# Gated channels one step ahead in a two-layer trunk: a change to the order of work in the first layer

## The chip, the cores and the metric

The kernel runs on one core of one Trainium2 chip. The metric is the device time of one execution in microseconds (us), lower is better. A run of this kernel gives one such time; the median of three runs stands for the kernel. One further execution was recorded with the hardware profiler, and all rows below come from it. Engine names follow the profile: PE is the matrix engine (PEld its weight loads), DVE the vector engine, ACT the scalar engine, POOL and SP the two others; SP issues most transfers and POOL issues the accumulating ones.

## The reference

The program is a trunk of two layers over 256 latent tokens and 256 context tokens of 1024 channels. Cut to what matters here, one layer does this:

```
h  = modulate(rmsnorm(x, norm1_g[l]), sh1, sc1)      # shifts and scales from silu(c) @ w_ada[l]
p  = h @ w_in[l]                                     # GLU columns | q k v | branch gates
u  = a * sigmoid(g)                                  # a, g: the two halves of the GLU columns
u  = dwconv1d(u, dw, dw_b)                           # depthwise, 31 taps, 512 channels
y_conv = silu(layernorm(u, ln_g, ln_b)) @ w_conv_out
y_attn = neighbourhood_attention(rope(q), rope(k), v, k_ctx, v_ctx, rpb) @ w_na_out
x  = x + g1 * ((sigmoid(pg_c) * y_conv + sigmoid(pg_a) * y_attn) @ w_out)
h2 = modulate(rmsnorm(x, norm2_g[l]), sh2, sc2)
x  = x + g2 * conv_ffn(h2)
```

The context tokens go through the same weights in the first layer with their own modulation and plain attention; in the second layer only their keys and values are needed. Weights and activations are float32. The kernel keeps that precision by splitting each operand into a high part and the rest and adding three products.

## The kernel before, in words

Channels lie on the 128 partitions and tokens on the free axis, 512 columns in the first layer (latent and context side by side). A **group** is one output tile of 128 channels: `group` runs over eight input tiles of 128 channels and `mm3` (lines 196 to 199) issues three matmuls for each, so a group is 24 matmuls into one of four PSUM banks tagged `main`. Its weights are one unit of 512 KB. `unit8` brings a unit in by one of two ways. `wadded` (lines 211 to 219) loads it on SP, lets ACT make the high part `whi` (line 216) and its negative `wlo` (217), and adds the loaded unit to that by an accumulating DMA from POOL (218). `wunit` (lines 157 to 180) lets ACT make `whi` (167) and DVE subtract it (168). A table at the top of the file, `ADDED`, says which unit goes which way; gates 5 and 7 of the first layer are not in it. There are four buffers each for the loaded unit (`raw`), `whi` and `wlo`.

The first layer's front runs in this order. Groups for the first GLU pair (which stand in two `sc` banks) and for the values end near 57 us. Then come, for each of four **pairs** of heads, a query group and a key group (`qk`, line 843), three further GLU pairs of two groups each (`glu_groups`, line 701), and sixteen gate groups (`gate`, line 708). After a query or key group DVE applies the rotary table (lines 859 to 869), ACT writes the high part (881) and DVE the low part (882). After a GLU pair ACT takes the tanh (691) and DVE the product (693), and 31 convolution **taps** per pair join a list; a tap is one DVE instruction over 512 columns (671 the first, 673 the others).

What is interleaved is set by generators. `group` calls `slot()` at its middle and at its end, and each slot advances every generator in `side`: `conv_run` (line 677) issues `rate` taps a slot; `Attention.run` steps the attention; `ada_dots` (line 289) issues the row sums, here called **dots**, that make the later modulation vectors: one DVE instruction over 128x1024 (line 304) for each of two token streams and each tile of `w_ada`, `pace` dots a slot. `layer_norm` (line 938) drains the taps, then sums the four channel tiles (949 to 951), has PE form the mean (955), and so on to the normal form (966 to 969).

The attention of a pair has three parts on PE: the scores (495), the transposes of the probabilities (561), and the values (578, 587). DVE takes the bias and the maximum (516), ACT the exponential (519) and the scaling (522); ACT copies the transposes out of PSUM (564, 567 for context). Latent scores of pair 0 are here called scores 0, and so on. `glu_groups(j)` calls `att.ahead(j - 2)`, which makes the attention issue the scores of all pairs up to that number; `qk(j)` does the same. A scheduler places the instructions of each engine in an order from this recording; each engine then runs its own list strictly in that order.

After the attention the tiles of its pool are free, and two 512 KB rows and the first `own` tiles for the dots are loaded into that space. The remaining gates follow, then eight half groups for the attention branch (`branch(U_NA, ...)`, DVE line 993), eight for the convolution branch (998, 999 and 1001 on DVE, 1000 on ACT) whose result `z` (tiles `h`) is the input of the output groups at line 1033. The dots of lines 933 and 1052 must be complete before the second norm.

Of the kernel before, what the change touches and what calls it, by code (L numbers as in the profile page):

```python
# [53 lines left out]
def trunk(ctx: ExitStack, tc: tile.TileContext, xt, cvec, crow, wall, wada, params, bias_t, rope_t, out):  # L54
# [13 lines left out]
    def nm(s):  # L68
        uid[0] += 1
        return f"{s}_{uid[0]}"  # L70
# [6 lines left out]
    def tmp(w=512):  # L77
        return tp.tile([P, w], F32, tag="t", bufs=5, name=nm("t"))
# [10 lines left out]
    def add_side(gen):  # L89
        side.append(gen)  # L90
# [196 lines left out]
    pace = [1.0]  # L287
# [344 lines left out]
    for l in range(DEPTH):  # L632
        last = l == DEPTH - 1
# [4 lines left out]
        with ExitStack() if last else start as e1a:  # L638
# [36 lines left out]
            rate = [0.0]  # L675
# [22 lines left out]
            def in_group(t, c, tag="main"):  # L698
                return group(psum(tag), unit8(l, U_IN + t), *h1, c)

            def glu_groups(j):
                pa = in_group(T_GLU + 2 * (j - 1), ALL)
                pg = in_group(T_GLU + 2 * (j - 1) + 1, ALL)
                copied = None if last else att.ahead(j - 2)
                with tc.issue_after(copied.ins) if copied else ExitStack():
                    glu(j, pa, pg)

# [5 lines left out]
            with ExitStack() as e1b:  # L713
# [3 lines left out]
                att = Attention(l, eb, T, V, VW, oh, ol, after)  # L717
# [125 lines left out]
                def qk(j):  # L843

                    att.ahead(j - 2)
                    bt = eb.tile([P, 5, NS_ // 2], F32, tag="bias", bufs=2 if last else 1, name=nm("bias"))
                    both = []
                    for what in range(2):
                        w = T if what == 0 else 2 * S
                        sc = HD ** -0.5 if what == 0 else 1.0  # L850
                        ps = in_group((T_Q, T_K)[what] + j, slice(0, w))
                        if what == 0:
                            with tc.issue_after(lastdma[0].ins):
                                sp.dma_start(bt, bias_t[l, j])
                        r1, r2 = tmp(), tmp()
                        got = back(ps[:, :w])
                        lat, ctx_ = (got[:, 0], got[:, 1]) if w > S else (got, None)
                        part = halves if w == S else lambda a: a
                        dve.tensor_tensor(part(r1[:, LAT]), lat, part(rope[:, 0, :]), ALU.mult)
                        dve.stream_shuffle(part(r2[:, LAT]), lat, SWAP16)  # L860
                        dve.tensor_tensor(r2[:, LAT], r2[:, LAT], rope[:, 1, :], ALU.mult)
                        if what == 0:
                            rq = tmp()
                            dve.tensor_tensor(
                                rq[:, LAT].rearrange("p (b r c) -> p b r c", b=NB_, r=ROWS),
                                blocks(r1[:, LAT]), blocks(r2[:, LAT]), ALU.add,
                            )
                        else:
                            dve.tensor_tensor(r1[:, LAT], r1[:, LAT], r2[:, LAT], ALU.add)
                        f = eb.tile([P, 2, KN if what else w], F32R, tag="qk"[what], bufs=2, name=nm("qk"))  # L870
                        if what == 0:
                            to = [([f[:, a, LAT] for a in range(2)], rq[:, LAT])]
                            if T > S:
                                to.append(([f[:, a, CTX] for a in range(2)], ctx_))
                        else:
                            rv_ = r1[:, LAT].rearrange("p (r c) -> p r c", r=ROWS)
                            to = [([f[:, a, KCTX] for a in range(2)], ctx_)]
                            for d, c in ((slice(0, KL), slice(GW - TC, GW)), (slice(KX, KN), slice(0, TC))):
                                to.append(([f[:, a, d].rearrange("p (c r) -> p r c", r=ROWS) for a in range(2)], rv_[:, :, c]))
                        for (hi, lo), src in to:  # L880
                            act.activation(hi, src, AF.Identity, scale=sc)
                            end = dve.scalar_tensor_tensor(lo, src, sc, hi.bitcast(F32), ALU.mult, ALU.subtract)  # L882
                        both.append(f)
                    att.pair(j, *both, bt, end)

                if l == 0:
                    for t in range(4):
                        keep_v(t, pv[t])
                    qk(0)
                    arun = att.run()  # L890
                    add_side(arun)
                    for j in range(1, 4):
                        glu_groups(j)
                        qk(j)
                        rate[0] = 3
                else:
                    glu_groups(2)
                    rate[0] = 3
                    wvs = [wunit(l, U_V + uu) for uu in range(4)]
                    for half in range(2):  # L900
                        pv = {t: psum() for t in (2 * half, 2 * half + 1)}
                        for k in range(KD):
                            v_tile(pv, wvs[k // 2], k, pv)
                            if k % 2:
                                slot()
                        for t, p in pv.items():
                            keep_v(t, p)
                    qk(0)
                    glu_groups(3)
                    arun = att.run()  # L910
                n = 0
                if last:
                    add_side(arun)
                    for j in range(1, 4):
                        gate(ea, n)
                        n += 1
                        qk(j)
                while att.busy() and n < (14 if last else 5):
                    gate(ea, n)
                    n += 1  # L920
                while att.busy():
# [3 lines left out]
            with ExitStack() as e1c:  # L925
                ec = e1c.enter_context(tc.tile_pool(name=f"ec{l}", bufs=1))

                if l == 0:
                    sb0 = [across(ec, s) for s in range(2)]

                    own = lambda: ec.tile([P, UW], F32, tag="own", bufs=4, name=nm("own"))
                    pace[0] = 0.5
                    g1 = ada_dots(0, range(16, 40), sb0, own, 2)
                    add_side(g1)
                sh_ = [ec.tile([P, T], F32R, name=f"sh{l}_{j}") for j in range(KC)]
# [2 lines left out]
                def layer_norm():  # L938

                    while taps:  # L940
                        for _ in range(6 if last else 5):
                            if taps:
                                conv_tap(*taps.pop(0))
                        yield
                    pace[0] = 1.0 if last else 1.2
                    flat = [c.rearrange("p s t -> p (s t)") for c in cb]
                    sm = tp.tile([P, 512], F32, tag="ss", name=nm("ss"))
                    eng = pool if last else dve
                    eng.tensor_tensor(sm[:, :T], flat[0], flat[1], ALU.add)
                    eng.tensor_tensor(sm[:, :T], sm[:, :T], flat[2], ALU.add)  # L950
                    dve.tensor_tensor(sm[:, :T], sm[:, :T], flat[3], ALU.add)
                    for _ in range(1 if last else 5):
                        yield
                    pm = psum("po")
                    pe.matmul(pm[:, :T], one.to_broadcast([P, P]), sm[:, :T], start=True, stop=True)
                    (s2,) = sum_squares(1, T)
                    for j in range(KC):
                        dve.scalar_tensor_tensor(flat[j], pm[:, :T], -1.0 / CONV, flat[j], ALU.mult, ALU.add)
                        s2.add(flat[j], j == KC - 1)
                    for _ in range(2 if last else 5):  # L960
                        yield
                    pb = yield from rstd(s2, CONV, "po", 0 if last else 2)
                    for j in range(KC):
                        sg = tmp()
                        g, b = pr(l, LNG + j, 1), pr(l, LNB + j, 1)
                        dve.scalar_tensor_tensor(flat[j], flat[j], g, pb[:, :T], ALU.mult, ALU.mult)
                        act.activation(sg[:, :T], flat[j], AF.Silu, bias=b)
                        act.copy(sh_[j], sg[:, :T])
                        dve.tensor_tensor(sl_[j], sg[:, :T], sh_[j].bitcast(F32), ALU.subtract)
                        yield  # L970
                    if last:
                        pace[0] = 0.4
# [384 lines left out]
```

## Time and profile before

| what | value |
|---|---|
| three runs | 1054.67, 1055.67, 1056.23 us |
| median | 1055.67 us |
| profiled execution, own time | 1054.58 us |
| its span, first to last instruction | 1052.8 us |
| PE, DVE, ACT busy in the span | 1032.4, 893.2, 565.6 us |
| taps (673) / dots (304) in the whole program | 240 / 128 |

The profiled execution's own time is 1.8 us above its span and 1.09 us below the median. In the page a group of instructions is one line of code on one engine with output and input tile names; a row of the timeline gives start, duration, engine, line, tiles and, in square brackets, how long the engine stood idle before it and what ended that. A 512-column matmul is recorded as 379 to 386 ns long, although one starts every 0.22 us: matmuls overlap, so PE's busy time hides short stalls.

### The profile page before, as it was taken

The page shows a single profiled execution, that of the slowest core. Times are in us where ns is not written, and L with a number is a line of the kernel's source. Part 1 is how long each engine was busy: PE and PEld are TensorE (multiplying, and loading weights), DVE is VectorE, ACT ScalarE, POOL GpSimd, SP SyncE. Part 2 cuts the span into 40 slices and gives each one's busy share as a digit, 9 for nine tenths or more (in the row PEclk, how much of TensorE's full clock was granted, in tenths as well). Part 3 has the DMA queues.
Part 4 walks back from the last instruction along what each step waited for, and adds up shares of the span by engine and source line. Part 5 has one row for each costly group of instructions (what it writes and reads, how often), then busy time and mean ns, then how long its engine had stood idle before and what let it go on. Part 6 is the DMA issues. An engine that isn't in the chain of part 4 may idle for free.

```text
span 1052.8 us, 17991 instructions
## 1 busy us (share of the span) xinstructions
PE 1032.4 (98%) x6886; PEld 932.9 (89%) x6886; DVE 893.2 (85%) x1608; ACT 565.6 (54%) x921; POOL 43.7 (4%) x59
## 2 busy tenths in 40 slices
PE   9999999999999999999999999999999999999997
PEld 7787788888889988888888889999889999999996
DVE  6568899999998787878788888799899988988883
ACT  4458768545434644444444223545777666766652
POOL 1111110011000000000000000000000000000000
PEclk9999999999999999999999999999999999999998
DMA  9989674888945345454545887556734485666781
GB/s 374 305 221 229 156 181 121 258 255 236 305 146 177 104 140 160 140 164 143 166 145 160 301 289 249 180 189 209 208 123 135 161 292 176 193 201 199 221 283 57
DMA packets 59511, 209.26 MB, mean 199 GB/s; under 512 B 7201, under 2 KB 7457, under 8 KB 59425
## 3 DMA queue, kind: packets, MB, share of 16 engines
q1 hardware_dynamic: 54384, 190.77, 55.3%
q0 software_dynamic: 4752, 17.30, 8.7%
q8 instruction: 54, 0.88, 0.3%
q14 instruction: 33, 0.26, 0.1%
q10 hardware_dynamic: 288, 0.04, 0.0%
HBM read 187.63 MB, written 1.05 MB: 179 GB/s over the span
## 4 chain that ended last, share of the span: by engine, by line
PE 68%; DVE 17%; ACT 5%; DMA 4%; issue 3%; SPq 1%; DVEq 0%; ACTq 0%
PE main L197 20%; PE main L198 20%; PE main L199 20%; DVE cb L673 6%; PE main L736 4%; DVE wlo L168 3%; DMA raw<-in_wall 2%; DVE t L304 2%; DMA own<-in_wada 1%; SPq L728 1%; PE sc L197 1%; PE sc L199 1%; PE sc L198 1%; DVE qk L882 1%; ACT pp L519 1%
## 5 line engine op out<-in xcount | busy, mean ns | idle before, releaser
L197 PE MATMUL main<-h,whi 128*128 128x256 f32 (+1 forms) x1328 | 433.1, 326 | 1.2 <-DVE qk L882 1.2
L198 PE MATMUL main<-h,whi 128*128 128x256 f32 (+1 forms) x1328 | 430.2, 324 | 0.9 <-DVE h L1001 0.7
L199 PE MATMUL main<-h,wlo 128*128 128x256 f32 (+1 forms) x1328 | 429.9, 324 | 1.2 <-DVE wlo L168 1.1
L167 ACT CAST whi<-raw 128x1024 fp32r<-128x1024 f32 (+1 forms) x211 | 218.3, 1039 | 234.8 <-PE main L198 173.6
L168 DVE TENSOR_TENSOR wlo<-raw,whi 128x1024 fp32r<-128x1024 f32 (+1 forms) x211 | 253.6, 1208 | 67.2 <-ACT whi L167 66.4
L197 PEld LDWEIGHTS main<-h,whi 128*128 128x128 f32 x1328 | 252.8, 190 | 22.0 <-issue 1.3
L199 PEld LDWEIGHTS main<-h,wlo 128*128 128x128 f32 x1328 | 252.5, 190 | 18.5 <-DVE wlo L168 1.8
L198 PEld LDWEIGHTS main<-h,whi 128*128 128x128 f32 x1328 | 252.7, 190 | 18.3 <-DVE h L1001 1.0
L304 DVE CUSTOM_DVE_ANT_0 t<-own,sb,par 128x1024 bf16<-128x1024 f32 x120 | 151.8, 1282 | 6.8 <-DMA own<-in_wada 6.8
L673 DVE SCALAR_TENSOR_TENSOR cb<-u,par,cb 128x512 f32<-128x512 f32 (+1 forms) x240 | 144.7, 620 | 2.8
L198 PE MATMUL main<-fl,whi 128*128 128x256 f32 (+1 forms) x396 | 122.8, 310 | 0.0
L197 PE MATMUL main<-fh,whi 128*128 128x256 f32 (+1 forms) x396 | 122.8, 310 | 0.0
L199 PE MATMUL main<-fh,wlo 128*128 128x256 f32 (+1 forms) x396 | 122.5, 310 | 0.0
L197 PEld LDWEIGHTS main<-fh,whi 128*128 128x128 f32 x396 | 75.6, 191 | 3.8 <-ACT fh L1095 0.2
L198 PEld LDWEIGHTS main<-fl,whi 128*128 128x128 f32 x396 | 75.6, 191 | 3.7 <-DVE fl L1096 0.2
L199 PEld LDWEIGHTS main<-fh,wlo 128*128 128x128 f32 x396 | 75.5, 191 | 3.6
L216 ACT CAST whi<-raw 128x1024 fp32r<-128x1024 f32 x33 | 34.6, 1049 | 36.0 <-PE main L198 30.5
L404 ACT ACTIVATE h<-t,mod 128x256 fp32r<-128x256 f32 x56 | 25.2, 503 | 34.8 <-DVE t L403 34.3
L218 POOL DMA_DIRECT2D wlo<-raw x33 | 28.9, 877 | 258.9 <-ACT wlo L217 107.6
L736 PE MATMUL main<-whi,h 128*128 128x512 f32 x128 | 38.5, 386 | 0.2
L1105 ACT ACTIVATE t<-t 128x512 f32<-128x512 f32 x22 | 13.9, 632 | 41.3 <-DVE t L1074 41.3
L217 ACT ACTIVATE wlo<-whi 128x1024 fp32r<-128x1024 f32 x33 | 35.0, 1061 | 0.5
(214 smaller groups left out, 1268.8 us busy)
## 6 DMA issues: line engine op xcount, KB each, us to landing
raw<-in_wall SPq DMA_DIRECT2D x240, 512.0 KB, 4.3
own<-in_wada SPq DMA_DIRECT2D x72, 512.0 KB, 4.7
wlo<-raw POOLq DMA_DIRECT2D x33, 512.0 KB, 5.4
raw<-in_wada SPq DMA_DIRECT2D x16, 512.0 KB, 5.8
bias<-in_bias_t SPq DMA_DIRECT2D x8, 520.0 KB, 5.3
row<-in_wada SPq DMA_DIRECT2D x8, 512.0 KB, 5.1
sb<-in_crow SPq DMA_DIRECT2D x5, 512.0 KB, 4.8
x<-in_xt SPq DMA_DIRECT2D x4, 512.0 KB, 5.1
```

The source lines that it names most:

```text
L167: act.copy(hi[:, c], r[:, c])
L168: dve.tensor_tensor(lo[:, c], r[:, c], hi[:, c].bitcast(F32), ALU.subtract)
L197: pe.matmul(ps, w[0], order(xh), start=start, stop=False)
L198: pe.matmul(ps, w[0], order(xl), start=False, stop=False)
L199: pe.matmul(ps, w[1], order(xh), start=False, stop=stop)
L216: act.copy(hi, r)
L217: act.mul(lo, hi.bitcast(F32), -1.0)
L218: pool.dma_start(lo, r, accum_op=ALU.add)
L304: dve.tensor_tensor_reduce(tmp().bitcast(BF16), r, v, 1.0, pr(l, BADA + n, 1), ALU.mult, ALU.add, mods[l][:, n, s : s + 1])
L404: high = act.activation(hi[:, c], y[:, c], AF.Identity, bias=b)
L673: dve.scalar_tensor_tensor(cb[j], src, w, cb[j], ALU.mult, ALU.add)
L736: mm = pe.matmul(pv[t], h1[n == 1][k][:, c], runs(w[n == 2][:, b]), start=k + n == 0, stop=k == KD - 1 and n == 2)
```

## The change

The first layer's order is altered in four ways, and the second layer's order is left as it is.

- GLU pair j+1 is computed ahead of query and key pair j: `glu_groups(1)` stands before `qk(0)`, and the loop runs `glu_groups(j + 1)` and `qk(j)` for j = 1, 2. `glu_groups` asks for the scores only up to pair j - 3. The last pair's queries and keys come behind the first gate, by the loop that the second layer used before.
- The taps go at three a slot beside GLU groups, two beside the queries and keys of pairs 2 and 3, one beside pair 1, and three beside pair 0. Before it was two up to the end of pair 1 and three after.
- Up to eight gates, not five, are taken while the attention is unfinished.
- The pace of the dots is 0.8 a slot, not 0.5, until the taps are drained, and 1.4, not 1.2, from there to the attention branch.

```diff
             def glu_groups(j):
                 pa = in_group(T_GLU + 2 * (j - 1), ALL)
                 pg = in_group(T_GLU + 2 * (j - 1) + 1, ALL)
-                copied = None if last else att.ahead(j - 2)
+                copied = None if last else att.ahead(j - 3)
...
                     att.ahead(j - 2)
+                    if not last:
+                        rate[0] = 1.0 if j == 1 else 2.0 if j else 3.0
...
                     att.pair(j, *both, bt, end)
+                    rate[0] = 3.0
...
+                    rate[0] = 3.0
+                    glu_groups(1)
                     qk(0)
                     arun = att.run()
                     add_side(arun)
-                    for j in range(1, 4):
-                        glu_groups(j)
+                    for j in range(1, 3):
+                        glu_groups(j + 1)
                         qk(j)
-                        rate[0] = 3
...
-                    for j in range(1, 4):
+                for j in range(1 if last else 3, 4):
+                    if True:
                         gate(ea, n)
                         n += 1
                         qk(j)
-                while att.busy() and n < (14 if last else 5):
+                while att.busy() and n < (14 if last else 8):
...
-                    pace[0] = 0.5
+                    pace[0] = 0.8
...
-                    pace[0] = 1.0 if last else 1.2
+                    pace[0] = 1.0 if last else 1.4
```

The change adds five lines up to there, so line 881 of before is line 883 of after, and 1001 is 1006. Three places show what it does to the engines' lists.

On ACT, the place is the stretch around the first pair's queries. Line 216 makes the high part of a weight unit, 217 its negative, 881 (883) the high part of queries or keys `qk`, 691 a tanh. Before:

```order
L216 CAST whi_897<-raw_895 128x1024
L217 ACTIVATE wlo_898<-whi_897 128x1024
L881 ACTIVATE qk_716<-main_672 128x256
L881 ACTIVATE qk_716<-t_714 128x256
L216 CAST whi_946<-raw_944 128x1024
L217 ACTIVATE wlo_947<-whi_946 128x1024
L881 ACTIVATE qk_763<-main_721 128x256
L881 ACTIVATE qk_763<-t_757 128x4x40 x2
L216 CAST whi_1028<-raw_1026 128x1024
```

The same place now, from the same ordinal unit (`raw_854` is the fifth of this run, as `raw_895` was) to the seventh and eighth:

```order
L216 CAST whi_856<-raw_854 128x1024
L217 ACTIVATE wlo_857<-whi_856 128x1024
L216 CAST whi_894<-raw_892 128x1024
L691 ACTIVATE t_747<-main_709 128x512
L217 ACTIVATE wlo_895<-whi_894 128x1024
L216 CAST whi_984<-raw_982 128x1024
L883 ACTIVATE qk_797<-main_751 128x256
L217 ACTIVATE wlo_985<-whi_984 128x1024
L883 ACTIVATE qk_797<-t_795 128x256
L216 CAST whi_1031<-raw_1029 128x1024
```

The high part of pair 0's queries stood ahead of the sixth unit and pair 0's keys ahead of the seventh; now both stand behind the cast of the seventh unit, `raw_982`. On SP the seventh load of this run stands, before and now, behind sixteen small transfers of line 728.

On PE, the place is the start of the output groups (line 1033). Their input `z` is eight tiles of 128 channels, each with a high and a low part, all named `h`. In before the last tile's parts are `h_2676` and `h_2684`, and `main_3044` and `main_3079` are the first and the second output group. Before, behind seven tiles of the first group and eleven matmuls of the second:

```order
L197 MATMUL main_3079<-h_2672,whi_3081 128x512
L198 MATMUL main_3079<-h_2680,whi_3081 128x512
L197 MATMUL main_3044<-h_2676,whi_3046 128x512
L199 MATMUL main_3079<-h_2672,wlo_3082 128x512
L197 MATMUL main_3079<-h_2673,whi_3081 128x512
L198 MATMUL main_3079<-h_2681,whi_3081 128x512
L199 MATMUL main_3079<-h_2673,wlo_3082 128x512
L197 MATMUL main_3079<-h_2674,whi_3081 128x512
L198 MATMUL main_3044<-h_2684,whi_3046 128x512
L199 MATMUL main_3044<-h_2676,wlo_3047 128x512
```

Now, where `main_3038` is the first output group and the last tile's parts are `h_2655` and `h_2663`:

```order
L197 MATMUL main_3038<-h_2654,whi_3040 128x512
L198 MATMUL main_3038<-h_2662,whi_3040 128x512
L199 MATMUL main_3038<-h_2654,wlo_3041 128x512
L197 MATMUL main_3038<-h_2655,whi_3040 128x512
L198 MATMUL main_3038<-h_2663,whi_3040 128x512
L199 MATMUL main_3038<-h_2655,wlo_3041 128x512
L197 MATMUL main_3079<-h_2648,whi_3081 128x512
L198 MATMUL main_3079<-h_2656,whi_3081 128x512
L199 MATMUL main_3079<-h_2648,wlo_3082 128x512
```

Before, the last low part was wanted by the 39th matmul of the output groups; now it is wanted by the 23rd, straight behind the seventh tile.

On DVE, the place is the end of the chain that makes those parts: line 998 (1003) multiplies a convolution group by its gate, 999 (1004) adds the attention branch, 1001 (1006) is the low part, 304 a dot and 168 the low part of a weight unit. Before:

```order
L1001 SCALAR_TENSOR_TENSOR h_2683<-t_3014,h_2675 128x512
L998 SCALAR_TENSOR_TENSOR t_3038<-g_7_2288,main_3019 128x512
L304 ISA t_3110,mod_105<-own_2963,sb_2143,par 128x1024
L304 ISA mod_105 128x1
L999 TENSOR_TENSOR t_3038<-t_3038,g_15_2667 128x512
L304 ISA t_3112,mod_105<-own_2963,sb_2146,par 128x1024
L304 ISA mod_105 128x1
L1001 SCALAR_TENSOR_TENSOR h_2684<-t_3038,h_2676 128x512
```

Now:

```order
L1004 TENSOR_TENSOR t_3014<-t_3014,g_14_2597 128x512
L168 TENSOR_TENSOR wlo_3082<-raw_3080,whi_3081 128x1024
L1003 SCALAR_TENSOR_TENSOR t_3032<-g_7_2274,main_3019 128x512
L1006 SCALAR_TENSOR_TENSOR h_2662<-t_3014,h_2654 128x512
L1004 TENSOR_TENSOR t_3032<-t_3032,g_15_2646 128x512
L304 ISA t_3057,mod_105<-own_2889,sb_2215,par 128x1024
L304 ISA mod_105 128x1
L1006 SCALAR_TENSOR_TENSOR h_2663<-t_3032,h_2655 128x512
```

Of the 48 dots that stand ahead of the second norm in both kernels, 40 stood ahead of the last low part before, and 37 do now. Ahead of the centred tiles of the layer norm (line 958, now 963) it was 6 and is 8, ahead of the normal form (966, now 971) 18 and 20; so 22 dots stood between the normal form and the last low part, and now 17.

Counted on PE, the mean of the layer norm (line 955, now 960) and all that follows it stands one and a half groups, 36 matmuls, later among the gate groups, so that as much less gate work lies between that mean and the output groups. From the second norm on, the lists of the two kernels agree.

## The prediction

> **What bounds the kernel now.** I read the page first.
>
> ```profile
> span 1052.8 us, 17991 instructions
> PE 1032.4 (98%) x6886; PEld 932.9 (89%) x6886; DVE 893.2 (85%) x1608; ACT 565.6 (54%) x921; POOL 43.7 (4%) x59
> ```
>
> PE is the bound, and the change gives it neither more nor fewer instructions. So the time can move only where PE waits or starts late. The second view is the table of stretches, cut at the layer's stages. Its columns are the stretch, its length, then busy time and count of PE, PEld, DVE, ACT and POOL, the granted clock, the share of the DMA engines and GB/s.
>
> ```profile
> 57.60:97.00 39.40, 38.02 (x201) 32.19 (x199) 31.66 (x72) 27.80 (x47) 6.83 (x8) 1.00 0.89 226
> 97.00:156.00 59.00, 56.60 (x396) 46.98 (x397) 54.12 (x119) 43.48 (x92) 6.93 (x8) 1.00 0.74 176
> 156.00:196.40 40.40, 40.27 (x289) 33.58 (x288) 36.93 (x66) 29.96 (x67) 2.62 (x3) 1.00 0.54 146
> 196.40:238.10 41.70, 40.73 (x191) 35.10 (x190) 38.75 (x59) 18.49 (x24) 4.63 (x4) 1.00 0.90 274
> 238.10:296.90 58.80, 58.14 (x271) 50.20 (x270) 56.05 (x89) 26.45 (x33) 5.26 (x6) 1.00 0.83 248
> 296.90:322.70 25.80, 25.80 (x177) 24.19 (x175) 23.01 (x49) 8.74 (x16) 0.00 (x0) 1.00 0.40 124
> 322.70:1052.80 730.10, 717.32 (x5011) 667.49 (x5009) 621.49 (x1077) 382.69 (x593) 10.36 (x15) 1.00 0.59 186
> 400.00:420.00 20.00, 20.00 (x94) 17.51 (x93) 16.49 (x24) 9.07 (x12) 0.00 (x0) 1.00 0.51 152
> ```
>
> From 57.6 to 296.9 us, where all moved work lies, PE idles 1.38 + 2.40 + 0.13 + 0.97 + 0.66 = 5.5 us: that is about all that better order can win. The last row is the measure of PE's step: 94 matmuls of 512 columns in 20.00 us, 0.213 each; with a few records missing I take 0.216, so a group of 24 is 5.2 us. DVE, at 80 to 95 per cent, is what PE waits for. The waits themselves are in PE's timeline:
>
> ```profile
> 96.04 0.44 PE L495 MATMUL sc<-qk,qk 64*128 64x416 f32 x2 [0.87 <-ACT qk L881]
> 97.07 0.62 PE L495 MATMUL sc<-qk,qk 64*128 64x416 f32 x4 [0.58 <-DVE qk L882]
> 104.61 0.27 PE L561 MATMUL pt<-ident,pp 64*128 64x64 f32 x1 [0.25 <-ACT pp L522]
> 128.60 1.28 PE L495 MATMUL sc<-qk,qk 64*128 64x416 f32 x6 [1.69 <-ACT pT L567]
> 213.02 1.12 PE L955 MATMUL po<-ss,one 128*128 128x512 f32 x2 [0.97 <-DVE ss L951]
> 287.83 0.38 PE L197 MATMUL main<-h,whi 128*128 128x512 f32 x1
> 292.85 0.48 PE L198 MATMUL main<-h,whi 128*128 128x512 f32 x1 [0.66 <-DVE h L1001]
> ```
>
> In order: scores 1 (1.45 in two pieces), a transpose (0.25), scores 2 (1.69), the layer norm's mean (0.97), the start of the output groups, and their wait for the low part of `z` (0.66). Together 5.0 us. I cost the change at each.
>
> **Scores 1.** Two more groups now stand ahead of them (of the pairs 2 and 3), so PE comes 10.4 us later: its first kind, due at 96.04 - 0.87 = 95.17, at 105.6, and the second kind, 0.44 behind, at 106.0. DVE's part by then:
>
> ```profile
> 59.19 3.12 DVE L673 SCALAR_TENSOR_TENSOR cb<-u,par,cb 128x512 f32<-128x512 f32 x4
> 138.29 1.42 DVE L673 SCALAR_TENSOR_TENSOR cb<-u,par,cb 128x512 f32<-128x512 f32 x2
> 139.61 0.69 DVE L693 SCALAR_TENSOR_TENSOR u<-t,main 128x512 f32<-128x512 f32 x1
> 140.21 2.75 DVE L673 SCALAR_TENSOR_TENSOR cb<-u,par,cb 128x512 f32<-128x512 f32 x4
> 77.84 0.60 DVE L516 CUSTOM_DVE_ANT_0 sc<-sc,bias 128x416 f32<-128x416 f32 x1 [3.29 <-PE sc L495]
> 80.60 0.69 DVE L693 SCALAR_TENSOR_TENSOR u<-t,main 128x512 f32<-128x512 f32 x1 [1.55 <-ACT t L691]
> 83.56 0.16 DVE L521 RECIPROCAL ri<-sm 128x1 f32<-128x1 f32 x1 [2.27 <-ACT pp L519]
> 96.20 0.81 DVE L882 SCALAR_TENSOR_TENSOR qk<-t,qk 128x160 fp32r<-128x160 f32 x2
> 77.00 1.05 ACT L216 CAST whi<-raw 128x1024 fp32r<-128x1024 f32 x1 [5.47 <-DMA raw<-in_wall]
> ```
>
> A tap that follows its own sum costs 3.12 / 4 = 0.78 us; where two sums alternate, two taps take 139.61 - 138.29 = 1.32, 0.66 each. With both kinds in the new list I take 0.72. Up to the last low part of pair 1's keys, which ended at 96.20 + 0.81 = 97.01, the new list holds 18 more taps (13.0), one product (139.61 to 140.21: 0.60) and one first tap (about 0.5): 14.0 us. Against that go idle times of 3.29, 1.55 and 2.27, 7.1 in all, in which DVE waited for PE and ACT; its new work covers them.
>
> A new wait comes on ACT. The cast of the seventh unit (77.00) waited 5.47 us for its load, with nothing behind it that was wanted. Now the high parts of pair 0's queries and keys stand behind that cast. DVE's low part of the queries waits for them, and behind it in DVE's list stand the taps and the keys; PE's scores 0 wait in turn. By my hand sum DVE would reach this low part near 75.8; ACT gives it near 78.2 (77.00 + 1.05 and a short activation): 2.4 us lost on DVE. Scores 0 have two groups of slack behind those, and come some 0.7 us before they would be late.
>
> So the keys are ready at 97.01 + 14.0 + 2.4 - 7.1 = 106.3, and PE, due at 106.0, waits 0.3 to 0.5 instead of 1.45: **-1.0**. Ends: -1.45, if taps run at 0.66 (1.1 less), and +1, if a third of the idle time stays.
>
> The Trainium skill has a rule against this ("VectorE: DVE Perf Modes", "The DRAIN you can't avoid"): the next operation does not start until the pipe is empty. By that rule alternating taps would cost what chained ones do, and 18 of them 14.0 us: scores 1 would wait 1.0 us more, and the term would be nil. The trace disagrees, 0.66 against 0.78, so I stay with the rows.
>
> **The transpose's 0.25** falls away: a GLU group (`G3a`) now fills that place as another did, but the scaling ahead of it is done sooner: -0.25, at worst 0.
>
> **Scores 2 and 3.** Both wait for ACT's copies of the context transposes, which free the banks.
>
> ```profile
> 125.91 1.07 ACT L216 CAST whi<-raw 128x1024 fp32r<-128x1024 f32 x1
> 127.02 1.06 ACT L217 ACTIVATE wlo<-whi 128x1024 fp32r<-128x1024 f32 x1
> 127.98 1.05 ACT L567 COPY pT<-sc 128x512 f32<-128x512 f32 x2
> 152.18 1.08 ACT L216 CAST whi<-raw 128x1024 fp32r<-128x1024 f32 x1
> 153.14 0.87 ACT L564 COPY pT<-sc 128x384 f32<-128x384 f32 x2
> 153.88 0.63 ACT L711 ACTIVATE g<-main 128x512 f32<-128x512 f32 x1
> ```
>
> Before scores 2 two conversions (2.1 us) stood ahead of the copies. Now the negative (1.06) stands behind them, one gate's tanh (0.63) ahead, and pair 2's queries come later: I take the copies 1.2 us sooner, **-1.2** (0 to -1.69). Before scores 3 one cast (1.08) stands ahead of the copies as before, yet PE comes there earlier by part of a group: **+0.8** (0 to +2).
>
> **The mean.** Its sum waits for the last tap. Taps now end sooner, at three a slot from the start, and the mean stands 36 matmuls (7.8 us) later on PE. The wait is gone: **-0.97**, with some 7 us to spare.
>
> **The output groups.** This is the price of the same move. The gates that lay between the mean and the output groups are 36 matmuls fewer, so PE gets there 287.83 - 213.02 - 7.8 = 67.0 us after the mean, and needs the last low part 22 matmuls on, at 71.8. DVE's chain between:
>
> ```profile
> 214.18 2.48 DVE L958 SCALAR_TENSOR_TENSOR cb<-po,cb 128x512 f32<-128x512 f32 x4
> 227.92 0.16 DVE L378 TENSOR_SCALAR red<-pt 128x4 f32<-128x4 f32 x1 [1.00 <-PE pt L370]
> 238.82 2.06 DVE L966 SCALAR_TENSOR_TENSOR cb<-cb,par,po 128x512 f32<-128x512 f32 x3 [2.44 <-PE po L386]
> 296.32 0.69 DVE L1001 SCALAR_TENSOR_TENSOR h<-t,h 128x512 fp32r<-128x512 f32 x1
> L168 DVE TENSOR_TENSOR wlo<-raw,whi 128x1024 fp32r<-128x1024 f32 x205 | 249.5, 1223 | 66.9 <-ACT whi L167 66.4 <-DMA raw<-in_wall 0.5
> L304 DVE CUSTOM_DVE_ANT_0 t<-own,sb,par 128x1024 bf16<-128x1024 f32 x120 | 151.8, 1282 | 6.8 <-DMA own<-in_wada 6.8
> ```
>
> It ended at 296.32 + 0.69 = 297.01, 84.0 after the mean. Of it go five dots (34 to 29 behind the centring, 5 x 1.22; a dot's 1.28 overlaps its neighbour a little) and one low part of a weight unit (1.22): 7.3. The waits of 1.00 and 2.44 for the layer norm's own steps stay. From 238.1 to 296.9 DVE idled 58.80 - 56.05 = 2.75, 0.7 of it the end of that 2.44; the other 2.0 were waits for PE, which a late DVE doesn't have. So the chain takes 84.0 - 7.3 - 2.0 = 74.7, and PE waits 74.7 - 71.8 = 2.9 us, plus a few tenths since the seventh tile's low part is late by about as much: 3.2. Less the 0.66 of before: **+2.5**. Ends: -0.66, if DVE has kept up with the convolution groups (then four short instructions and a dot lie behind PE's last one, and `z` comes with PE), and +3.5.
>
> **Behind that** three dots and a weight's low part, 4.9 us, must be done ahead of the second norm that were done sooner before. DVE had 25.80 - 23.01 = 2.8 us free there, and comes there 74.7 - 84.0 + 7.8 = 1.5 us earlier in PE's frame: 0.6 us short, which the second norm's own waits take up: 0 (to +1.5). In the rest, 730 us, both kernels have the same list: 0.
>
> **Sum:** -1.0 - 0.25 - 1.2 + 0.8 - 0.97 + 2.5 + 0 = -0.1, from the profiled execution's 1054.58 to 1054.5. That execution is 1.09 under the median, so in medians 1055.5. A measurement of this kernel can tell about 0.2 per cent, 2.1 us, from no change.
>
> **Rivals.**
> - *The front's waits go and `z` is in time.* All of scores 1, the transpose, scores 2 and the mean come to 1.45 + 0.25 + 1.69 + 0.97 = 4.4, of which scores 3 takes a little back: 4.1 us faster, 1051.5. For it: DVE is free for 7 us before the mean, and the dots that it takes there are off the chain. Against it: the list itself puts the last tile straight behind the seventh. Chance 0.35, with what lies between it and the forecast by more than 2.1.
> - *The change moves nothing*: the waits go where they were by other names. Then 1055.7; chance 0.06, inside the forecast's 0.44.
> - *Slower: the seventh load.* It decides if that load lands more than about 0.7 us later than at 77.00: from there each microsecond goes through the cast, the queries' high part, DVE and scores 0 or 1 to PE. Its issue stands on SP behind sixteen transfers of line 728 and the bias loads behind two more units, with the DMA engines 89 per cent busy in that stretch. Landing 3.3 us later costs 2.6: 1058.1. Chance 0.16; another 0.02 for a `z` wait at its upper end with scores 3 at theirs.
> - *The clock.* The longest PE wait among the moved ones is 1.69 and the granted clock is 1.00 in every stretch; a wait of 3.2 us has no row here. If PE came back from it at half rate for as long again, it would lose 1.6 us: 1057.1, or 1058 with a late load; chance 0.03. The Trainium skill ("TensorE: Matmul & The Clock Gate", "Part 1: The HAM clock gate (the "warmup" mystery)") puts the idle window that lowers the clock at about 3.4 us, just above my estimate; no row here shows it.
>
> **The numbers.** The forecast, within 2.1 us either way, has 0.44, faster 0.35, slower 0.21. The range reaches from the first rival with `z` fully in time (1055.67 - 4.4 - 0.4, about 1050.9) to the load 3.3 us late (1058.2).
>
> **What would show it.** Right: PE's wait for `h` from line 1006 grows to about 3 us near the output groups' start, no wait at line 960, under 0.6 us at scores 1, and ACT's wait for `raw` ahead of line 883. Wrong in size: no wait at line 1006 (then DVE had kept up), or a DVE idle time at 516 that stays. Wrong in kind: new PE waits at scores 0, or any stretch with a clock below 1.00.

## The result and the profile after

Twelve runs of each kernel in turn gave 1052.82 us (median, 1051.28 to 1055.81) against 1056.04 us before: a ratio of 0.9971, 95% interval 0.9961 to 0.9981, so about 3.1 us faster (2.0 to 4.1). The change was run again later beside other kernels and gave the same ratio, 0.9971 (0.9956 to 0.9986). That lies in the predicted range, but not in the case that was called the likeliest (within 2.1 us): it lies between that and the rival that gave 4.1 us. One execution of a kernel below (the pace alone) took 1522 us at a granted clock of 0.65 throughout, and no comparison uses it.

The first profile of the changed kernel was of the slowest of these twelve executions (1055.81 us), for a reason that it shows itself, below. So I read it beside a second one (1052.57 us), called "again" here. PE's timeline of the first, at six places: scores 0, scores 1, scores 2, the mean, the attention branch and the output groups.

```profile
87.70 1.19 PE L495 MATMUL sc<-qk,qk 64*128 64x416 f32 x6 [0.30 <-ACT qk L883]
107.66 1.20 PE L495 MATMUL sc<-qk,qk 64*128 64x416 f32 x6 [1.41 <-ACT qk L883]
139.16 1.10 PE L495 MATMUL sc<-qk,qk 64*128 64x416 f32 x5 [0.42 <-ACT pT L567]
219.41 1.02 PE L960 MATMUL po<-ss,one 128*128 128x512 f32 x2
251.66 0.48 PE L199 MATMUL main<-oh,wlo 128*128 128x512 f32 x1 [0.98 <-DMA wlo<-raw]
293.09 0.48 PE L198 MATMUL main<-h,whi 128*128 128x512 f32 x1 [0.59 <-DVE h L1006]
```

The waits at the mean and at one transpose are gone, that of scores 2 went from 1.69 to 0.42, and scores 1 and `z` wait about as long as before (1.41 for 1.45, 0.59 for 0.66). At `z` it isn't the same tile, though: before, PE waited at the 20th matmul of the output groups, for the seventh tile's low part, and now at the 23rd, for the last one's. Two waits are new: 0.30 at scores 0, and 0.98 in the attention branch. The brackets don't hold everything. Six score matmuls take 1.19 and 1.20 us here at scores 0 and 1, and 0.80 in a run below where nothing waits; the expectations below name 0.7 and 2.0 us for these two waits.

PE's sum to about the 23rd matmul of the output groups stands in the table of stretches, first of "again", then of before:

```profile
57.60:291.40 233.80, 230.15 (x1328) 195.20 (x1326) 213.47 (x397) 145.64 (x261) 26.30 (x29) 1.00 0.77 214
```

```profile
57.60:293.30 235.70, 230.15 (x1326) 195.22 (x1325) 213.91 (x397) 145.55 (x259) 26.27 (x29) 1.00 0.79 215
```

PE is busy for the same 230.15 us in both, and idle for 3.65 instead of 5.55. The first stretch ends 0.12 us inside the wait for `z`, so the saving there is 1.8 us. The own times of these two executions, in both of which the clock stayed up to 1040 us, differ by 2.0 us (1054.58 to 1052.57). What makes up the rest of the 3.1 us is open. Two executions of one kernel without a fall of the clock can differ by 1.0 us (1051.28 and 1050.24, of the kernel in the first experiment), and the fastest runs of the two kernels lie 3.4 us apart here (1054.67 and 1051.28) and 3.1 beside the experiments (1053.95 and 1050.90).

The clock is one candidate. This is the first profile of the changed kernel, microsecond by microsecond around its wait at scores 1; the clock is the third number from the end.

```profile
106.00:107.00 1.00, 0.24 (x2) 0.00 (x0) 1.00 (x3) 1.00 (x2) 0.00 (x0) 1.00 0.02 4
107.00:108.00 1.00, 0.34 (x2) 0.19 (x2) 0.77 (x3) 1.00 (x3) 0.65 (x1) 1.00 0.63 33
108.00:109.00 1.00, 0.87 (x10) 0.77 (x10) 0.29 (x2) 0.97 (x2) 0.22 (x1) 1.00 0.57 180
109.00:110.00 1.00, 1.00 (x8) 0.68 (x5) 1.00 (x4) 0.96 (x2) 0.05 (x1) 0.81 0.94 328
110.00:111.00 1.00, 1.00 (x4) 0.77 (x3) 0.78 (x6) 1.00 (x5) 0.81 (x1) 0.50 1.14 246
111.00:112.00 1.00, 1.00 (x4) 0.82 (x3) 1.00 (x6) 1.00 (x3) 0.00 (x0) 0.50 1.03 205
112.00:113.00 1.00, 1.00 (x3) 0.77 (x3) 0.96 (x3) 1.00 (x4) 0.00 (x0) 0.50 1.05 205
113.00:114.00 1.00, 1.00 (x6) 0.85 (x5) 1.00 (x5) 0.78 (x4) 0.00 (x0) 0.98 1.09 217
```

PE idles 1.55 us between 106 and 109, and about a microsecond later its clock stands at a half for 3.4 us: three or four matmuls begun or running in a microsecond instead of six. The same happened behind an idle 1.5 us near 869 us, in code that the change doesn't touch. "Again" has both waits too (1.41 and 1.33 in its rows) and no fall. The two executions differ by 1055.81 - 1052.57 = 3.2 us, 1.6 a fall; half of 3.4 us is 1.7.

### The profile page after: what moved, and what is told of

It is laid out like the page before. It is cut to its first block, busy times and chain, and to the rows that moved or that the text cites. A ratio compares the mean times of both kernels' runs of the same rounds, so it can differ in the third digit from the quotient of the medians.

```text
span 1054.0 us, 17988 instructions
## 1 busy us (share of the span) xinstructions
PE 1034.6 (98%) x6886; PEld 935.0 (89%) x6886; DVE 893.9 (85%) x1608; ACT 564.1 (54%) x921; POOL 43.3 (4%) x59
## 4 chain that ended last, share of the span: by engine, by line
PE 78%; DVE 10%; DMA 4%; ACT 4%; issue 3%; SPq 1%; POOL 0%; DVEq 0%; ACTq 0%; POOLq 0%
PE main L197 22%; PE main L198 22%; PE main L199 22%; PE main L736 4%; DMA raw<-in_wall 2%; DVE cb L673 2%; DVE wlo L168 2%; PE sc L199 1%; PE sc L197 1%; PE sc L198 1%; DMA wlo<-raw 1%; ACT whi L167 1%; DVE qk L884 1%; PE po L578 1%; PE po L230 1%
```

## The experiments

**The seventh unit behind the queries.** The first profile showed the blocked queries of the prediction, made longer by a late load that only a rival had named. ACT's and DVE's timelines of the changed kernel:

```profile
78.55 1.05 ACT L216 CAST whi<-raw 128x1024 fp32r<-128x1024 f32 x1 [9.56 <-DMA raw<-in_wall]
79.50 0.38 ACT L883 ACTIVATE qk<-main 128x256 fp32r<-128x256 f32 x1
```

```profile
79.91 0.42 DVE L884 SCALAR_TENSOR_TENSOR qk<-main,qk 128x256 fp32r<-128x256 f32 x1 [3.65 <-ACT qk L883]
```

The load lands at 78.5 instead of 77.0, ACT holds the queries' high part behind it, and DVE stands for 3.65 us. The experiment puts that cast behind the queries' two high parts, and leaves all else:

```diff
+    behind = []
     def wadded(l, u):
...
-        act.copy(hi, r)
+        with ExitStack() as es:
+            for b in behind:
+                es.enter_context(tc.issue_after(b.ins))
+            act.copy(hi, r)
...
+                        behind[:] = first if not last and j == 1 and what == 0 else []
                         ps = in_group((T_Q, T_K)[what] + j, slice(0, w))
+                        behind[:] = []
```

(`first` holds the two high parts of pair 0's queries.)

> The changed kernel with one thing altered: ACT's cast of the seventh weight unit is placed behind the high parts of pair 0's queries instead of ahead of them. Theory A (the late load blocks ACT, and through it DVE and PE): DVE's idle time of 3.65 us ahead of the queries' low part falls below 0.5, scores 0 wait nothing (0.7 before), scores 1 wait 0.5 us or less (2.0), and the time falls by 1.5 to 3 us below the changed kernel, to about 1050.5 us. Theory B (DVE is behind with its taps anyway, the idle time is only refilled): scores 1 still wait 1.5 us or more and the time moves by less than 0.7 us.

It gave 1051.28 us, ratio 0.9939 (0.9925 to 0.9954). PE, ACT and DVE of this run:

```profile
88.99 0.80 PE L500 MATMUL sc<-qk,qk 64*128 64x416 f32 x6
107.07 0.80 PE L500 MATMUL sc<-qk,qk 64*128 64x416 f32 x6
```

```profile
77.02 0.38 ACT L892 ACTIVATE qk<-main 128x256 fp32r<-128x256 f32 x1 [6.37 <-issue]
78.61 0.42 ACT L892 ACTIVATE qk<-t 128x256 fp32r<-128x256 f32 x1 [1.21 <-DVE t L875]
78.93 1.03 ACT L221 CAST whi<-raw 128x1024 fp32r<-128x1024 f32 x1
```

```profile
77.83 0.41 DVE L895 SCALAR_TENSOR_TENSOR qk<-main,qk 128x256 fp32r<-128x256 f32 x1
```

The cast now starts right behind the queries' second high part, and blocks neither; DVE doesn't wait, and the waits at scores 0 and 1 have no brackets any more. Theory A holds, with a gain of 3.4 us by the two ratios, a little above its 3: the cast that waits for the late load is what kept scores 1 late. The same kernel, run on one chip with the experiment on the attention branch below:

> The kernel with the seventh unit behind the queries once more, on one chip with the next one. Theory A: 0.6 per cent below before again, with mean clocks of 0.997 or more in all runs, since no PE wait over 1 us is left up to 300 us. Theory B (the first call's ratio was luck): within 0.1 per cent of the changed kernel's ratio of 0.9971.

It gave 1050.76 us, ratio 0.9943 (0.9922 to 0.9964), so the gain came again; its mean clocks were 0.995 to 0.998, not all as high as expected.

**The pace of the dots, undone.**

```diff
-                    pace[0] = 0.8
+                    pace[0] = 0.5
...
-                    pace[0] = 1.0 if last else 1.4
+                    pace[0] = 1.0 if last else 1.2
```

> The changed kernel with the dots' pace as before (0.5 and 1.2). Counted in DVE's list, 6 dots instead of 8 stand ahead of the centring, 36 instead of 37 ahead of the last low part of z, so 30 instead of 29 between them. Theory A (the new wait of 0.98 us in the attention branch is the price of the higher pace, whose loads crowd the accumulating transfer; it hides most of the z wait): that transfer takes 5 to 6 us instead of 9.4 and the wait goes, the z wait grows from 0.6 to 2 us or more, and the time is within 1 us of the changed kernel. Theory B (the wait has another cause, such as the cast's place): the transfer takes 8 us or more still, the wait stays, and with the z wait a little longer the time is up to 1.2 us longer.

It gave 1061.80 us, ratio 1.0051 (1.0034 to 1.0068): slower than before, and some 8 us above the changed kernel. Neither theory had that. The accumulating transfer took 9.7 us at the lower pace too and the attention branch waited 1.31, so the higher pace isn't what makes it long, and theory A is out; but most of the 8 us lies elsewhere, at the second norm. DVE's list there, and what PE waits for behind it:

```profile
320.14 1.28 DVE L304 CUSTOM_DVE_ANT_0 t<-own,sb,par 128x1024 bf16<-128x1024 f32 x1
321.35 1.28 DVE L304 CUSTOM_DVE_ANT_0 t<-own,sb,par 128x1024 bf16<-128x1024 f32 x1
322.55 1.28 DVE L304 CUSTOM_DVE_ANT_0 t<-own,sb,par 128x1024 bf16<-128x1024 f32 x1
323.76 1.28 DVE L304 CUSTOM_DVE_ANT_0 t<-own,sb,par 128x1024 bf16<-128x1024 f32 x1
324.96 1.28 DVE L304 CUSTOM_DVE_ANT_0 t<-own,sb,par 128x1024 bf16<-128x1024 f32 x1
326.17 0.15 DVE L378 TENSOR_SCALAR red<-pt 128x2 f32<-128x2 f32 x1
```

```profile
337.38 0.58 PE L199 MATMUL sc<-h,wlo 128*128 128x256 f32 x1 [5.39 <-DVE wlo L168]
```

Five dots in a row stand ahead of the norm's reciprocal root (378), where the changed kernel has one; the low parts of the next weights come late by it, and PE stands 5.4 us. The clock is at a half from 335.8 to 342.6 us, 5.3 us of it behind the wait, which costs 2.6 more. I read it so that the new order and the higher pace belong together: the new order leaves less gate work behind the mean, and the dots must have been done ahead of it.

**The taps' rates, undone** (two a slot to the end of pair 1, three from there).

> The changed kernel with the taps' rates as before (two a slot to the end of pair 1, then three). PE's order stays as in the changed kernel. Theory A (taps at three a slot are what overfills DVE ahead of scores 0 and 1): fewer taps stand ahead of pair 1's keys, scores 1 wait under 1 us instead of 2.0, the mean still waits for nothing since it had some 7 us to spare, and the time is 0.5 to 2 us below the changed kernel. Theory B (the rate is what brings the mean in time): the mean waits 1 us or more again and the time is 1 us or more above the changed kernel.

1054.61 us, ratio 0.9977 (0.9968 to 0.9986): not to be told from the changed kernel's 0.9971. Scores 0 and 1 wait for nothing, the mean neither, as theory A has it; but nothing was won, because other waits grew. Scores 3 wait 0.54 us, a transpose 0.95 and a gate 0.36, and scores 2 again more:

```profile
138.15 1.11 PE L495 MATMUL sc<-qk,qk 64*128 64x416 f32 x5 [1.08 <-ACT pT L567]
```

So the taps' new rates bring no gain that these runs can tell.

**At most five gates beside the attention, as before.**

> The changed kernel with at most five gates taken while the attention is unfinished, as before. Theory A (the extra gates are only cover: with two gate groups fewer beside it the attention's last part runs bare, and the mean comes earlier again): PE waits 2 to 5 us more near the attention's end, the mean stands half a group earlier, and the time is 2 to 5 us above the changed kernel. Theory B (the limit decides nothing, since the attention ends by seven gates anyway): the time is within 1 us of the changed kernel.

1073.91 us, ratio 1.0170 (1.0147 to 1.0193): worse than either theory. Near the attention's end PE waits 1.40 us for one transpose, less than theory A's 2 to 5. Most is lost behind it, where the gates stand that are no longer beside it: PE waits 2.68 us for a weight's low part, 1.80 for the mean's sum and, in the attention branch, 3.38 for an accumulating transfer and 3.21 for another, and the clock falls near 211, 262 and 279 us:

```profile
209.69 0.48 PE L199 MATMUL main<-h,wlo 128*128 128x512 f32 x1 [2.68 <-DVE wlo L168]
222.94 1.12 PE L960 MATMUL po<-ss,one 128*128 128x512 f32 x2 [1.80 <-DVE ss L956]
262.60 0.79 PE L199 MATMUL main<-oh,wlo 128*128 128x512 f32 x1 [3.38 <-DMA wlo<-raw]
```

**The changed kernel again.**

> The changed kernel, unaltered, beside the others of this call and with a new profile, since the clock fell twice in its first one. Theory A: the waits at scores 0 and 1, in the attention branch and at z come again with nearly the same sizes (about 0.7, 2.0, 1.0 and 0.6 us), and the clock stays at 1.00 in some profiles after scores 1 and not in others; the time is about 3 us below before. Theory B: the waits at scores 0 and 1 were made by the fall of the clock, and are under 1 us together when the clock stays up.

1052.91 us, ratio 0.9971 (0.9956 to 0.9986). Theory A: the wait of 1.41 at scores 1, 0.43 at scores 2 and 0.59 at `z` are there again, with no fall of the clock between 60 and 1040 us; scores 0 show no bracket this time. So the wait at scores 1 isn't made by the fall.

**The pace alone, on the kernel before.** The edit is the reverse of the second one, on the old order.

> The kernel before with the new pace of the dots alone (0.8 and 1.4). Counted in DVE's list, 9 dots instead of 6 stand ahead of the sum for the mean, and 43 instead of 40 ahead of the last low part of z. Theory A (the pace pays only because the taps now end early): the mean waits 0.97 + 3 x 1.2 = 4.6 us, and the time is 2 to 4 us above before. Theory B (the pace is what brings the gain): the time is 1 us or more below before.

Three runs gave 1068.45, 1072.24 and 1073.09 us, ratio 1.0140 (1.0118 to 1.0163), far beyond theory A. The recorded execution was the one of 1522 us, so its profile is left aside for another:

> The kernel before with the new pace alone once more, for a profile (the first one was taken at a clock of 0.65). Theory A (too many dots ahead of weights' low parts and of the mean's sum, as in the run with five gates): PE waits over 2 us for line 168 in the gates, over 2 us for the mean's sum, and over 2 us for weights in the attention branch, and the clock falls behind some of these waits; together 12 to 16 us. Theory B (the mean's wait alone): 4 to 5 us there, and the rest from the clock.

That one took 1068.98 us. PE's waits that the kernel before has not, or not so long, then ACT's and POOL's rows that explain the last:

```profile
209.50 0.48 PE L199 MATMUL main<-h,wlo 128*128 128x512 f32 x1 [1.07 <-DVE wlo L168]
215.71 1.13 PE L955 MATMUL po<-ss,one 128*128 128x512 f32 x2 [1.19 <-DVE ss L951]
240.77 0.48 PE L199 MATMUL main<-h,wlo 128*128 128x512 f32 x1 [1.89 <-DMA wlo<-raw]
273.76 0.80 PE L199 MATMUL main<-oh,wlo 128*128 128x512 f32 x1 [3.18 <-DMA wlo<-raw]
```

```profile
264.22 2.96 ACT L217 ACTIVATE wlo<-whi 128x1024 fp32r<-128x1024 f32 x3
```

```profile
265.68 2.77 POOL L218 DMA_DIRECT2D wlo<-raw  x3 [23.63 <-ACT wlo L217]
```

Theory A has the places and the total right: 1068.98 is 13.4 us above the profiled 1055.57 of before, below. Not all of the sizes are: two waits are smaller than expected (1.07 and 1.19, not over 2), and the four rows make 7.3 us together. The clock stood at a half for 3.4 us near 99 and 242, and for 6.8 us from 272.6, 5.7 of it behind the last wait. By half of each that is 6.2 us more. The longest wait seems to come from a step that I hadn't named: three negatives (217) stand together in ACT's list, and with them three accumulating transfers start within 2.8 us and take 10.6 us (median) to land. Why the scheduler puts them so is open. What holds is that the pace alone is a loss of 1.4%.

**The second unit of the attention branch made by DVE**, on the kernel with the seventh unit behind the queries. That unit's accumulating transfer took 9.4 us in the changed kernel and 5.4 before.

```diff
-for u in (U_NA + 1, U_NA + 3,
+for u in (U_NA + 3,
```

> The kernel with the seventh unit behind the queries, and in it the second unit of the attention branch made by DVE (line 168 of before) instead of the accumulating transfer. DVE has one low part of a weight unit (1.2 us) more ahead of z. Theory A (the wait in the attention branch hid a z wait, because DVE's chain decides): the branch's wait of 0.67 goes, z waits 0.58 + 0.67 + 1.2 = 2.4 us, and the time is 0.5 to 1.5 us longer than without this edit. Theory B (DVE has kept up with the convolution groups, and z follows PE): z waits 0.6 as before and the time falls by 0.5 us or more.

> The kernel with the attention branch's second unit made by DVE as well, on one chip with the run ahead. Theory A (the wait in the branch only moved to z and to the second norm): within 0.5 us of the run ahead. Theory B (that wait was on the path): 0.6 us or more below it.

1049.99 us, ratio 0.9939 (0.9927 to 0.9951), and 1049.98 us, 0.9929 (0.9912 to 0.9946), beside 1050.76 for the kernel without it on the same chip. The wait in the branch is gone; PE waits 0.27 and 0.66 us at the output groups, not 2.4:

```profile
287.24 0.48 PE L197 MATMUL main<-h,whi 128*128 128x512 f32 x1 [0.27 <-ACT h L1016]
288.38 0.48 PE L198 MATMUL main<-h,whi 128*128 128x512 f32 x1 [0.66 <-DVE h L1017]
```

The first call's theory A falls: in the list, the added low part stands ahead of the normal form, where DVE idles anyway. Whether the edit gains is unclear: the second run lies 0.78 us below, as its theory B has it, but the intervals overlap and the kernel without the edit showed no wait in the branch either. It is the fastest kernel of the study, by a hair.

**Three taps a slot beside pair 1 too.**

```diff
-                        rate[0] = 1.0 if j == 1 else 2.0 if j else 3.0
+                        rate[0] = 2.0 if j > 1 else 3.0
```

> The changed kernel with three taps a slot beside pair 1's queries and keys too, not one. Two more taps stand ahead of pair 1's last low part and seven more ahead of pair 2's. Theory A (the lower rate is there to bring these keys in time): scores 1 wait 1.4 us more, scores 2 become late by some us, and the time is 1.5 to 5 us above the changed kernel. Theory B (it only moves taps about): the time is within 1 us of the changed kernel.

1055.13 us, ratio 0.9988 (0.9978 to 0.9998): 2.2 us above the changed kernel's median of 1052.91 beside it, though the two intervals overlap. Scores 1 now wait 1.72 + 0.47, 0.8 us more, and two transposes 0.40 and 0.72; scores 2, which theory A had late, don't wait at all. So the time is near theory A's lower end, and its mechanism holds for scores 1 alone, at about half its size.

**The kernel before again.**

> The kernel before, unaltered, for a second profile: its timed runs show mean granted clocks of 0.995 to 0.996 mostly, the first profile 0.997. Theory A (in most executions the clock falls behind one of its PE waits of 1.5 to 2 us): a stretch of some 4 us at half clock behind scores 1, scores 2 or the wait near 869 us. Theory B (the lower mean comes from elsewhere, the start or the end): no stretch below 1.00 between 60 and 1040 us.

1055.57 us. Theory A's stretch is there; that it comes in most executions one profile can't show. Here is the clock around scores 2:

```profile
127.00:128.00 1.00, 0.28 (x10) 0.14 (x6) 1.00 (x3) 0.97 (x2) 0.00 (x0) 1.00 0.82 123
128.00:129.00 1.00, 0.04 (x1) 0.04 (x1) 0.93 (x3) 1.00 (x3) 0.16 (x1) 1.00 0.99 401
129.00:130.00 1.00, 0.95 (x7) 0.68 (x8) 0.96 (x2) 1.00 (x3) 0.70 (x1) 1.00 0.78 160
130.00:131.00 1.00, 1.00 (x9) 0.70 (x6) 0.96 (x2) 0.64 (x2) 0.00 (x0) 0.56 0.71 164
131.00:132.00 1.00, 1.00 (x4) 0.71 (x3) 1.00 (x5) 0.00 (x0) 0.00 (x0) 0.50 0.97 324
```

An idle 1.7 us, and from 130.1 on the clock at a half for 3.4 us. The profile that the prediction rests on had the same wait and no fall. The waits of one kernel vary, too: scores 1 wait 1.41 + 0.58 us here, not 0.87 + 0.58, and the mean 0.30, not 0.97.

## Why the prediction was right or wrong

**The number: in the range, by luck in part.** By the brackets of the first profile the terms were wrong by +1.0 (scores 1), +0.3 (scores 0), -0.8 (scores 3), +1.0 (the attention branch) and -2.6 (`z`). They cancel in part, down to about -1.1 us, and the range is 7 us wide. Of the prediction's own signs, those of being wrong in kind came: a wait at scores 0 and stretches with the clock below 1.00. Those of being right came for the mean and for ACT's wait, but not for `z` and scores 1.

**The bound and its size: right.** PE's idle time from 57.6 us to the output groups was put at 5.5 us and all gain sought there; it went from 5.55 to about 3.8.

**Scores 1, -1.0: wrong, it was 0,** with 0.3 lost at scores 0 in the first profile. (Against the second profile of before it is -0.6.) The step that failed is "ACT gives it near 78.2": the load landed 1.5 us later than in the kernel before, ACT gave the high part at 79.9, and DVE lost 3.65 us, not 2.4. This is the rival of the seventh load, in part: it set its point of decision 0.7 us behind 77.00, and the load came 1.5 behind. The first experiment shows that cause, and that undoing it is worth about 0.3% of the time (0.9939 and 0.9943 against 0.9971), more than the waits at scores 0 and 1 by themselves; where the rest comes from is open.

**The transpose, scores 2 and the mean: right.** -0.25, -1.27 (1.69 to 0.42, forecast -1.2) and -0.97 (-0.30 against the second profile of before). **Scores 3, +0.8: wrong, nothing;** no wait shows there in either profile.

**`z`, +2.5: wrong, it was -0.07,** and this is the largest part of the miss. The mechanism was named rightly, the term mis-sized from two sides. DVE's chain from the normal form on:

```profile
245.11 2.07 DVE L971 SCALAR_TENSOR_TENSOR cb<-cb,par,po 128x512 f32<-128x512 f32 x3 [2.21 <-PE po L386]
...
292.35 0.68 DVE L1006 SCALAR_TENSOR_TENSOR h<-t,h 128x512 fp32r<-128x512 f32 x1
```

It takes 293.03 - 245.11 = 47.9 us, and took 297.01 - 238.82 = 58.2: 10.3 less, by five dots (6.1), two low parts of weights (2.4) and 1.6 us less idle time (2.03 to 0.40 in the stretches). "Of it go five dots and one low part" counted from the centring on. But one of the low parts had only moved ahead of the normal form, where DVE waits 2.21 us for PE in any case, and so costs nothing. That is 1.2 us: the last low part came 293.03 - 219.41 = 73.6 us after the mean, not 74.7. And PE came later: `z` was due 293.09 - 0.59 - 219.41 = 73.1 us after the mean, not 71.8, and 0.98 of these 1.3 us is PE's wait in the attention branch. That wait was in no part of the prediction.

**Behind that, 0: right for this change, but on an edge.** With the pace undone, five dots stand in a row ahead of the norm, and most of some 8 us is lost there.

**The clock: right to name, wrong as a rival of this change alone.** It was given 0.03, on a wait of 3.2 us that had no row. It falls behind waits of 1.5 to 1.7 us, in some executions of both kernels. Whether the kernel before falls more often is not shown. Mean clocks of 0.997 and more stand in 5 of the 49 runs of before that were made beside the experiments and in 16 of the 24 runs of the changed kernel, which points that way. But the mean also counts the end of the execution, where PE has little or nothing to do and the clock stands at a half: the kernel of the first experiment had a mean of 0.996 in the execution of 1050.24 us, without any fall between 60 and 1040 us. Nor is the profile of before shown to be a favourable one: of the two profiles of each kernel, one has no fall. The Trainium skill ("TensorE: Matmul & The Clock Gate", "Part 1: The HAM clock gate (the "warmup" mystery)") has the clock set by windows of about 3.4 us, of which one must be idle. The 3.4 us of these falls agree with the length; but idle times of half that length were enough in some executions, and there the measurement decides.

**The taps' cost: right.** Alternating and chained taps were taken at 0.72 us on average; the thirteen behind 59.35 in the changed kernel's timeline take 10.21 us, 0.78 each, all of one sum, and five alternating ones 3.40, 0.68 each:

```profile
59.35 10.21 DVE L673 SCALAR_TENSOR_TENSOR cb<-u,par,cb 128x512 f32<-128x512 f32 x13
...
71.19 3.40 DVE L673 SCALAR_TENSOR_TENSOR cb<-u,par,cb 128x512 f32<-128x512 f32 x5
```

## What to carry to other kernels

When work is moved ahead on one engine, look at what its weights' conversions on another engine will then stand in front of: a cast that waits for a late load is harmless only as long as nothing behind it is wanted, and one ordering edge was worth about as much as the change itself. When a chain's cost is counted by what leaves it, count from the last point where it waits for somebody else, not from its start: what moves ahead of that point is free as long as that wait outlasts it. And a rate that is good in one order can be a loss in another (the same pace cost 1.4% on the old order and its lack 0.8% on the new), so such numbers are to be tried together. No run here moves the GLU pairs alone, so what that part of the change is worth by itself is open.

## What the runs showed of the hardware

- The clock fell to a half for 3.4 us, roughly one microsecond behind PE idle times of 1.5 to 1.7 us, in some executions and not in others with the same wait; it cost about 1.6 us each time. Around idle times of 5.4 and 3.2 us it stood at a half for 6.8 us (the pace undone, and the pace alone), but for 3.4 us around idle times of 3.4 and 3.2 us (five gates).
- The accumulating transfer of one unit, 512 KB, took 5.4 us from issue to landing in the kernel before and 9.4 us in the changed one, 9.7 with its pace undone. Eight such transfers between 205 and 285 us took 5.2 to 10.3 us in the kernel before and 5.8 to 9.8 us in the changed one.
